# Moving six expert blocks of a mixture layer's first product from the dense stage into the stage before it

## The chip, the cores and the metric

One core of a Trainium2 chip runs the whole program. The metric is device time in microseconds (us) of one execution; the runs of a kernel are summed up by their median. The engines are named as the profile names them: PE (TensorE matmul) with PEld (its weight loads), DVE (VectorE), ACT (ScalarE), POOL (GpSimd) and SP (SyncE, which here only issues DMAs). Each engine takes its instructions in the order in which the program emits them.

## The reference

A bidirectional encoder block over 1024 tokens of width 1024: attention and a convolution side by side, then a retrieval layer with 16,384 experts, then a norm. Only the retrieval layer matters here. For each token, 8 heads pick 16 experts each, and the layer adds their outputs:

```
u = peer_u[e]
h = jax.nn.gelu(jnp.einsum('cd,chkd->chk', xc, u))
return jnp.einsum('chk,chkd->cd', g * h, peer_v[e])
```

`e` are the chosen experts of a token, found by two top-16 searches per head over 128 keys each and one over the candidate pairs; `g` is the softmax of the scores. All data are float32.

## The kernel before, in words

The 1024 tokens are 8 tiles of 128. Three tiles (`NG = 3`, 384 tokens) take the layer literally: for each of the 128 chosen experts of a token POOL issues an indirect DMA that fetches a row of `peer_u` or of `peer_v` per token (`rows` or `rx`, 128 rows of 4 KB), and DVE multiplies and adds it (L1195 for u, L1207 for v). That is 3 x 128 x 2 = 768 such gathers, each with one DVE instruction. Seven row buffers are in turn.

The other five tiles (640 tokens, `TD`) are computed densely. The experts are 128 blocks of 128. For a block i the first product is `gelu(peer_u[i] x HN)` (float32 split in a high and a low part, three products, so 48 matmuls of 320 columns; `HN` holds the 640 tokens), which is multiplied by a dense matrix of weights (`GD`, zero where a token has not chosen the expert) and multiplied with `peer_v[i]` (second product, 10 pieces of 128 tokens x 512 columns). Two stages concern us.

**The stage before the dense one** (the loop at L1410 on). Each turn of the loop does one group of the dense weights (`gpe`: eight matmuls `pg`, L1108, 160 groups in all; ACT evacuates them to `gblk`, and a DMA puts them into `GD` in DRAM after every eight groups) and one quarter of a first-product block (`ustep`: 12 matmuls, L1244). The finished block goes to DRAM (`HDm`). 31 blocks are made so (`KM = K0 - KT`, `K0 = 33`, `KT = 2`). With each turn `kadv` gives the top-16 searches and the gathers a credit of the turn's planned length, `max(dt + 1.4, 2.6)` with dt = 1.65 when a quarter was done and 0 otherwise; a gather costs 3.0 (`GCOST`), a step of the search what its generator yields. When the blocks are out the loop goes on with groups alone.

**The dense stage** starts with the two blocks left over (`KT`) and the loads for block 0. Then an iteration for each of blocks 0 to 126 does: loads for later blocks; `vsplit` of the next block's `peer_v` (ACT high part `vh`, POOL low part `vl`, L119); `uahead` (split of a `peer_uT` block for a first product to come, ACT and POOL, `uh` and `ul`, and the next load of one); and then three slots. A slot has a `rotate` (six matmuls into the one PSUM bank `prot`, which DVE then adds to X, L1569), `accum` (three matmuls in slots 1 and 2, six in slot 3, into four banks that stay), `ugroup` (12 matmuls, a quarter of a first product made here) and a few gathers. In the second slot `amake1` and `amake2` make the next block's left operand (DVE, `ho * gl`, L1487; ACT `ah`; DVE `al`). Of the 128 blocks 33 come back from `HDm` (`hload`); the other 95 are `ulist`, 380 quarters, one in each of 381 slots. SP issues all plain loads in the order of emission: `hload`, the `GD` slices `gl` (`gload`, every fourth block, both halves at once, three buffers), `vr` (`vload`), `ur` (`uload`).

Of the kernel before, what the change touches and what calls it, by code (L numbers as in the profile page):

```python
# [10 lines left out]
BF = mybir.dt.bfloat16  # L11
# [3 lines left out]
ALU = mybir.AluOpType  # L15
# [16 lines left out]
NK = 128  # L32
# [7 lines left out]
TB = 32  # L40
GCH = 4
NPERS = 4
K0 = 33
WIN = 2
NVI = 3
NO2 = 2
GPE = 1.4
GCOST = 3.0
KT = 2
GLAST = 1  # L50
FD = 2
# [20 lines left out]
def peer_block(tc, I, out):  # L72
    nc = tc.nc
    ctx = ExitStack()
    V, A, G, PE, SY = nc.vector, nc.scalar, nc.gpsimd, nc.tensor, nc.sync
# [1049 lines left out]
    class Gather:  # L1125
# [51 lines left out]
        def adv(self, n=1):  # L1177
            for _ in range(n):
                if not self.ready():
                    return  # L1180
                self.fill()
                ph, t, k = self.seq[self.nc]
                r = self.rows.pop(self.nc)
                self.nc += 1
                ps = self.ps
                if ph == 0:
                    h = self.h(t) if ps is None else ps
                    if k == 0:
                        self.hh[t] = gp.tile([P, P], F32, name=f"hh{t}")
                        if ps is not None:  # L1190
                            self.stage(t)
                            A.copy(ps, self.staged[t])
                            self.slots.append(self.staged.pop(t))
                    jk = QB[:, 2, :].bitcast(BF)
                    V.scalar_tensor_tensor(jk, r, 1.0, h, op0=ALU.mult, op1=ALU.mult,  # L1195
                                           accum_out=self.hh[t][:, k:k + 1])
                else:
                    if k == 0:
                        aa = gp.tile([P, P], F32, name=f"aa{t}")
                        A.activation(aa[:], self.hh[t][:], AF.Gelu_apprx_tanh)  # L1200
                        V.tensor_tensor(aa[:], aa[:], gg[t][:], op=ALU.mult)
                        self.aa[t] = aa
                    xt = X[:, t, :]
                    if k == 0 and ps is not None:
                        A.copy(ps, xt)
                    to = xt if ps is None else ps
                    V.scalar_tensor_tensor(to, r, self.aa[t][:, k:k + 1], to, op0=ALU.mult, op1=ALU.add)  # L1207
                    if k == P - 1 and ps is not None:
                        A.copy(xt, ps)
                self.slots.append(r)  # L1210
                if ph and k == P - 4 and t + 1 < NG and ps is not None:
                    self.stage(t + 1)
# [80 lines left out]
    def k_gat():  # L1293
        if not ks.get("gat") or not gat.ready():
            return None
        gat.adv(1)
        return GCOST

    def kstep():
        order = [("gen", k_gen), ("topk1", k_topk1), ("gat", k_gat)]  # L1300
# [49 lines left out]

    ust = dict(i=0, seg=0, hps=None, prev=None)

    def ustep():
        i = ust["i"]
        if i >= KM:
            return 0.0
        if i == 0 and ust["seg"] == 0:
            uload(US[0])
            uload(US[1])
            usplit(US[0])  # L1360
        sg = ust["seg"]
        if sg == 0:
            ust["hps"] = hbank([P, 2, 512], "hps")
        useg(US[i], ust["hps"], 2 * sg, 2 * sg + 2)
        if sg == 1 and ust["prev"] is not None:
            ho = gelu_(ust["prev"], up, 1)
            SY.dma_start(HDm[i - 1], ho[:])
        if sg == 1 and i < KM:
            usplit(US[i + 1])
            if i + 2 < K0:  # L1370
                uload(US[i + 2])
        ust["seg"] += 1
        if ust["seg"] == 4:
            ust["seg"] = 0
            ust["i"] += 1
            ust["prev"] = ust["hps"]
        return 1.65
# [34 lines left out]
    while True:  # L1412
# [4 lines left out]
            break  # L1417
        dt = max(dt + GPE * did, KB)
        kadv(dt, dt)
    ho = gelu_(ust["prev"], up, 1)  # L1420
    SY.dma_start(HDm[KM - 1], ho[:])
    while ks["n2"] < len(korder):
        clk["t"] += 2.0
        kstep()
# [2 lines left out]
    with ExitStack() as vs:  # L1427
# [27 lines left out]
        AL = {}  # L1455
        HO = {}

        def gload(i):
            for hf in range(2):
                gl[i, hf] = vp.tile([P, NB2, GCH, TB], F32, name="gl", tag="gl", bufs=3)  # L1460
                SY.dma_start(gl[i, hf][:], GD[hf * NB2:(hf + 1) * NB2, :, i:i + GCH, :].rearrange("b p i t -> p b i t"))

# [10 lines left out]
            CH[i] = (vh, vl)  # L1473

        hfree = [vp.tile([P, TD], F32, name=f"ho{j}")[:] for j in range(2)]
        hfree.append(QB[:, 0:2, :].rearrange("p a b -> p (a b)")[:, :TD])

        def hload(i):
            if i in UI and i not in HO and i < NK:
# [35 lines left out]

        def loads(i):
            if 0 <= i < NK:
                if i % GCH == 0:
                    gload(i)
                vload(i)  # L1520


        ulist = [i for i in range(NK) if i not in UI]
        ug = dict(g=0, split=0, load=0, ps=None)

        def uahead():
            m = ug["g"] // 4
            if ug["split"] < min(m + 2, len(ulist)):
                usplit(ulist[ug["split"]])
                ug["split"] += 1  # L1530
                if ug["load"] < len(ulist):
                    uload(ulist[ug["load"]])
                    ug["load"] += 1

        def ugroup():
            m, q = divmod(ug["g"], 4)
            if m >= len(ulist):
                return
            i, (hf, d) = ulist[m], divmod(q, 2)
            if ug["split"] <= m:  # L1540
                uahead()
            if d == 0:
                ug["ps"] = ubank()
            uhalf(i, hf, ug["ps"], d * DC // 2, (d + 1) * DC // 2)
            if d == 1:
                if hf == 0:
                    HO[i] = hfree.pop(0)
                ugelu(HO[i], hf, ug["ps"])
            ug["g"] += 1

        def uready(i):
            while i not in UI and ulist.index(i) >= ug["g"] // 4:
# [25 lines left out]
        ug["load"] = 2  # L1578
        hload(0)
        loads(0)  # L1580
        loads(1)
        for i in range(KM, K0):
            if i + 1 < K0:
                usplit(US[i + 1])
# [23 lines left out]
        for i in range(NK - 1):  # L1608
            nx = i + 1
            ng = gat0 + -(-(ngat - gat0) * min(nx, nb) // nb) - gat.nc  # L1610
            gs = [0] * 3
            for j in range(ng):
                gs[SPOTS[j % len(SPOTS)]] += 1
            hload(nx)
            if len(hfree) > 1:
                hload(i + 2)
            loads(i + 2)
            vsplit(nx)
            uahead()
            rs_ = [w for w in range(len(rot)) if i % WIN == w % WIN]  # L1620
            rotate(rs_[0], i, False)
            accum(i, (0,))
            ugroup()
            gat.adv(gs[0])
            rotate(rs_[1], i, False)
            accum(i, (1,))
            ugroup()
            uready(nx)
            amake1(nx)
            gat.adv(gs[1])  # L1630
            amake2(nx)
            rotate(rs_[2], i, False)
            accum(i, (2, 3))
            ugroup()
            gat.adv(gs[2])
            CH.pop(i - WIN, None)
        accum(NK - 1, range(len(pers)))
# [71 lines left out]
```

## Time and profile before

| | |
|---|---|
| runs, us | 2976.93 median of 3 (2971.88 to 2979.38) |
| profiled execution, us | 2979.52, its span 2977.7 |
| PE busy, share of the span | 94% |
| DVE busy | 81% |
| POOL busy | 64% |
| ACT busy | 39% |

A busy share is an average over stages; what a change in one of them is worth is read from that stage. Matmuls are pipelined, so that the durations of neighbouring ones overlap, and their spacing is less than their duration.

### The profile page before, as it was taken

The page shows a single profiled execution, that of the slowest core. Times are in us where ns is not written, and L with a number is a line of the kernel's source. Part 1 is how long each engine was busy: PE and PEld are TensorE (multiplying, and loading weights), DVE is VectorE, ACT ScalarE, POOL GpSimd, SP SyncE. Part 2 cuts the span into 40 slices and gives each one's busy share as a digit, 9 for nine tenths or more (in the row PEclk, how much of TensorE's full clock was granted, in tenths as well). Part 3 has the DMA queues.
Part 4 walks back from the last instruction along what each step waited for, and adds up shares of the span by engine and source line. Part 5 has one row for each costly group of instructions (what it writes and reads, how often), then busy time and mean ns, then how long its engine had stood idle before and what let it go on. Part 6 is the DMA issues. An engine that isn't in the chain of part 4 may idle for free.

```text
span 2977.7 us, 44502 instructions
## 1 busy us (share of the span) xinstructions
PE 2799.5 (94%) x16042; PEld 2477.2 (83%) x16048; DVE 2424.8 (81%) x4465; ACT 1166.3 (39%) x2408; POOL 1916.8 (64%) x1526
## 2 busy tenths in 40 slices
PE   7988899999999899978999999999999999999997
PEld 6867787798988788857888888888888888888886
DVE  4889877458666977766899988999889989898998
ACT  3237666243577577672222222222222222222222
POOL 2667741104446666765777777878777878787775
PEclk9999999899999999999999999999999999999999
DMA  3121000154345667668989898999989998999896
GB/s 124 53 76 36 1 15 1 53 161 122 96 149 181 224 219 251 235 238 299 342 331 350 328 348 331 345 342 352 337 319 337 344 343 336 347 336 339 332 342 227
DMA packets 296719, 710.33 MB, mean 239 GB/s; under 512 B 25264, under 2 KB 135216, under 8 KB 296368
## 3 DMA queue, kind: packets, MB, share of 16 engines
q0 software_dynamic: 110592, 402.70, 35.3%
q1 hardware_dynamic: 156800, 252.85, 25.2%
q10 hardware_dynamic: 29104, 51.91, 4.7%
q8 instruction: 126, 2.06, 0.3%
q14 instruction: 97, 0.79, 0.1%
HBM read 640.46 MB, written 66.91 MB: 238 GB/s over the span
## 4 chain that ended last, share of the span: by engine, by line
PE 53%; DVE 20%; DMA 11%; issue 7%; ACT 4%; POOL 4%; ACTq 1%; SPq 0%; POOLq 0%; DVEq 0%
PE hps L1504 13%; PE hps L1244 5%; PE prot L122 4%; PE prot L123 4%; PE prot L124 4%; DMA rows<-peer_u,ei 4%; PE pg L1108 3%; DMA rows<-peer_v,ei 2%; PE acc L124 2%; PE acc L122 2%; PE acc L123 2%; DMA vr<-peer_v 2%; DVE ga L1207 2%; DVE ho L1487 2%; DMA GD<-gblk 2%
## 5 line engine op out<-in xcount | busy, mean ns | idle before, releaser
L1504 PE MATMUL hps<-HN,uh 128*128 128x320 f32 x3072 | 682.8, 309 | 9.3 <-ACT ho L1251 5.3
L1504 PEld LDWEIGHTS hps<-HN,uh 128*128 128x128 f32 x3072 | 530.3, 188 | 42.7 <-issue 5.5
L1504 PE MATMUL hps<-HN,ul 128*128 128x320 f32 x1536 | 475.4, 309 | 0.6 <-POOL ul L119 0.6
L1207 DVE SCALAR_TENSOR_TENSOR ga<-rows,aa,ga 128x1024 f32<-128x1024 f32 x330 | 423.8, 1284 | 30.1 <-DMA rows<-peer_v,ei 23.6
L1162 POOL DMA_INDIRECT rows<-peer_u,ei x339 | 362.4, 1069 | 108.0 <-issue 56.3
L119 POOL TENSOR_TENSOR vl<-vr,vh 128x1024 fp32r<-128x1024 f32 x128 | 308.9, 2413 | 153.3 <-ACT vh L116 110.7
L1162 POOL DMA_INDIRECT rows<-peer_v,ei x330 | 325.2, 985 | 112.9 <-issue 64.5
L1195 DVE SCALAR_TENSOR_TENSOR QB<-rows,ga 128x1024 bf16<-128x1024 f32 x271 | 329.4, 1216 | 29.8 <-DMA rows<-peer_u,ei 25.5
L122 PE MATMUL prot<-vh,ah 128*128 128x512 f32 x762 | 308.8, 405 | 30.4 <-DVE X L1569 27.9
L119 POOL TENSOR_TENSOR ul<-ur,uh 128x1024 fp32r<-128x1024 f32 x127 | 323.0, 2543 | 2.6
L1569 DVE TENSOR_TENSOR X<-X,prot 128x512 f32<-128x512 f32 x384 | 261.9, 682 | 68.6 <-PE prot L124 66.4
L123 PE MATMUL prot<-vl,ah 128*128 128x512 f32 x762 | 301.0, 395 | 0.4 <-POOL vl L119 0.4
L124 PE MATMUL prot<-vh,al 128*128 128x512 f32 x762 | 297.4, 390 | 0.0
L1504 PEld LDWEIGHTS hps<-HN,ul 128*128 128x128 f32 x1536 | 289.1, 188 | 0.9 <-POOL ul L119 0.9
L1514 ACT ACTIVATE ho<-hps 128x320 f32<-128x320 f32 x128 | 55.9, 437 | 487.2 <-PE hps L1504 487.2
L1118 ACT COPY gblk<-pg 128x128 f32<-128x128 f32 x640 | 176.0, 441 | 100.6 <-PE pg L1108 71.4
L116 ACT CAST vh<-vr 128x1024 fp32r<-128x1024 f32 x128 | 133.7, 1045 | 201.7 <-DMA vr<-peer_v 201.7
L1244 PE MATMUL hps<-HN,uh 128*128 128x320 f32 x992 | 210.8, 335 | 0.0
L124 PE MATMUL acc<-vh,al 128*128 128x512 f32 x512 | 199.8, 390 | 0.0
L122 PE MATMUL acc<-vh,ah 128*128 128x512 f32 x512 | 199.8, 390 | 0.0
L123 PE MATMUL acc<-vl,ah 128*128 128x512 f32 x512 | 199.7, 390 | 0.0
L122 PEld LDWEIGHTS prot<-vh,ah 128*128 128x128 f32 x762 | 143.0, 188 | 67.9 <-DVE X L1569 47.6
(276 smaller groups left out, 6502.9 us busy)
## 6 DMA issues: line engine op xcount, KB each, us to landing
ur<-peer_uT SPq DMA_DIRECT2D x128, 512.0 KB, 4.4
vr<-peer_v SPq DMA_DIRECT2D x128, 512.0 KB, 7.8
GD<-gblk ACTq DMA_DIRECT2D x80, 512.0 KB, 5.1
gl<-GD SPq DMA_DIRECT2D x64, 640.0 KB, 7.7
wqr<-peer_wq SPq DMA_DIRECT2D x32, 512.0 KB, 3.9
HDm<-ho SPq DMA_DIRECT2D x31, 320.0 KB, 2.9
s<-SD SPq DMA_DIRECT2D x64, 128.0 KB, 3.0
ho<-HDm SPq DMA_DIRECT2D x22, 320.0 KB, 5.0
```

The lines of the kernel that those rows point to most:

```text
L116: A.copy(hi, src)
L119: lo_eng.tensor_tensor(lo, src, f(hi), op=ALU.subtract)
L122: PE.matmul(ps, ah, bh, start=start, stop=False)
L123: PE.matmul(ps, ah, bl, start=False, stop=False)
L124: PE.matmul(ps, al, bh, start=False, stop=stop)
L1118: A.copy(gblk[b][k][:, :, q * 4:q * 4 + 4].rearrange("p i t -> p t i"), pg[:, :, k * w:k * w + w])
L1162: G.indirect_dma_start(out=r, out_offset=None, in_=I["peer_v" if ph else "peer_u"], in_offset=bass.IndirectOffsetOnAxis(ap=ge[t][:, k:k + ...
L1195: V.scalar_tensor_tensor(jk, r, 1.0, h, op0=ALU.mult, op1=ALU.mult, accum_out=self.hh[t][:, k:k + 1])
L1207: V.scalar_tensor_tensor(to, r, self.aa[t][:, k:k + 1], to, op0=ALU.mult, op1=ALU.add)
L1244: PE.matmul(hps[:, j, :b - a], (uh, uh, ul)[st3][:, dc, :], HN[(0, 1, 0)[st3]][:, dc, a:b], start=dc == 0 and st3 == 0, stop=dc == DC - 1 ...
L1504: PE.matmul(ps[:, :b - a], (uh, uh, ul)[st3][:, dc, :], HN[(0, 1, 0)[st3]][:, dc, a:b], start=dc == 0 and st3 == 0, stop=dc == DC - 1 and ...
L1569: V.tensor_tensor(X[:, NG + t, n:n + 512], X[:, NG + t, n:n + 512], pr, op=ALU.add)
```

## The change

`K0` becomes 39, so 37 blocks are made in the loop of the stage before and 89 in the dense stage. A gather that is emitted after the last top-16 search costs 2.0 of credit instead of 3.0 (`GCOST2`). The product that L1195 writes beside its sum goes over the row itself instead of into a part of `QB`; with the space that this frees there are four buffers for finished blocks (`hfree`) instead of three. The last gelu of the loop is emitted in it (`ulast`). In the dense stage `gload` no longer stands ahead of `vload`: each half is loaded by itself, behind the `amake1` that reads the old one for the last time; `uload` stands behind `vload`; `uahead` splits behind the first quarter of a block; and the 356 quarters are spread over the 381 slots (`uslot`).

```
-K0 = 33
+K0 = 39
+GCOST2 = 2.0
...
-                    jk = QB[:, 2, :].bitcast(BF)
-                    V.scalar_tensor_tensor(jk, r, 1.0, h, op0=ALU.mult, op1=ALU.mult,
+                    V.scalar_tensor_tensor(r, r, 1.0, h, op0=ALU.mult, op1=ALU.mult,
                                            accum_out=self.hh[t][:, k:k + 1])
...
-        return GCOST
+        return GCOST if ks["n2"] < len(korder) else GCOST2
...
+    def ulast():
+        if ust["prev"] is not None:
+            ho = gelu_(ust["prev"], up, 1)
+            SY.dma_start(HDm[KM - 1], ho[:])
+            ust["prev"] = None
+
     def ustep():
         i = ust["i"]
         if i >= KM:
+            ulast()
             return 0.0
...
-        def gload(i):
-            for hf in range(2):
+        def gload(i, hf):
+            if i < NK:
...
-        hfree.append(QB[:, 0:2, :].rearrange("p a b -> p (a b)")[:, :TD])
+        hfree += [QB[:].rearrange("p a b -> p (a b)")[:, j * TD:(j + 1) * TD] for j in range(2)]
...
         def loads(i):
             if 0 <= i < NK:
-                if i % GCH == 0:
-                    gload(i)
                 vload(i)
...
         def uahead():
             m = ug["g"] // 4
             if ug["split"] < min(m + 2, len(ulist)):
                 usplit(ulist[ug["split"]])
                 ug["split"] += 1
-                if ug["load"] < len(ulist):
-                    uload(ulist[ug["load"]])
-                    ug["load"] += 1
+
+        def uloads():
+            if ug["load"] < min(ug["split"] + 2, len(ulist)):
+                uload(ulist[ug["load"]])
+                ug["load"] += 1
...
             ug["g"] += 1
+            if q == 0:
+                uahead()
+
+        def uslot():
+            ug["slot"] += 1
+            if ug["g"] < -(-4 * len(ulist) * ug["slot"] // (3 * (NK - 1))) and (ug["g"] % 4 != 1 or len(hfree) > 1):
+                ugroup()
...
         loads(0)
+        gload(0, 0)
+        gload(0, 1)
         loads(1)
+        gload(GCH, 0)
...
             hload(nx)
+            loads(i + 2)
             if len(hfree) > 1:
                 hload(i + 2)
-            loads(i + 2)
+            uloads()
             vsplit(nx)
-            uahead()
...
             amake1(nx)
+            if nx % GCH == GCH - 1:
+                gload(nx + 1, 1)
+                gload(nx + 1 + GCH, 0)
...
-            ugroup()
+            uslot()
```

(The last pair stands in each of the three slots.)

## Rows read from the trace of the kernel before

**Rows 1.** Stages: length, busy time of each engine (instructions), clock, DMA share, GB/s.

```profile
839.00:1277.60 438.60, 418.27 (x2843) 376.96 (x2843) 334.66 (x1199) 310.92 (x869) 284.24 (x230) 0.99 0.60 211
...
1277.60:1338.90 61.30, 44.25 (x260) 31.60 (x258) 38.61 (x50) 44.90 (x140) 33.99 (x22) 0.92 0.70 251
1338.90:1361.50 22.60, 16.10 (x96) 15.88 (x97) 3.04 (x4) 9.12 (x16) 1.56 (x1) 0.85 0.77 265
1361.50:2947.00 1585.50, 1559.79 (x8352) 1379.55 (x8353) 1427.54 (x1775) 387.98 (x547) 1232.71 (x918) 1.00 0.91 337
1900.00:2100.00 200.00, 199.95 (x1079) 177.78 (x1078) 181.98 (x270) 49.50 (x71) 159.25 (x120) 1.00 0.92 344
```

**Rows 2.** One quarter of a first product in the chain that ended last (start, us).

```profile
895.30 1.75 PE hps L1244 x12
```

**Rows 3.** Matmuls of the dense weights from 1140, and those from 1277.6 on.

```profile
L1108 PE MATMUL pg<-o,o x317: 270/275/275, 1139.8 to 1275.2; 128*128 128x128 f32 x159
...
L1108 PE MATMUL pg<-o,o x192: 270/275/582, 1277.7 to 1338.4; 128*128 128x128 f32 x192
```

**Rows 4.** A wait from 1277.6 to 1338.9: total us, times, longest.

```profile
PE pg L1108 <- ACT gblk L1118: 9.1, 2, 7.3
```

**Rows 5.** Gathers on DVE from 1277 to 1345 (ns min/median/max, first and last start).

```profile
L1195 DVE SCALAR_TENSOR_TENSOR QB<-rows,QB x17: 1214/1224/1226, 1277.1 to 1318.2; 128x1024 bf16<-128x1024 f32 x17
```

**Rows 6.** Dense stage by line: busy us, mean ns, idle before.

```profile
L1207 DVE SCALAR_TENSOR_TENSOR ga<-rows,aa,ga 128x1024 f32<-128x1024 f32 x327 | 419.9, 1284 | 30.1 <-DMA rows<-peer_v,ei 23.6 <-ACT ga L1205 1.5
...
L1569 DVE TENSOR_TENSOR X<-X,prot 128x512 f32<-128x512 f32 x380 | 259.1, 682 | 68.6 <-PE prot L124 66.4
...
L1487 DVE TENSOR_TENSOR ho<-ho,gl 128x320 f32<-128x320 f32 x169 | 172.3, 1058 | 3.0 <-DMA ho<-HDm 3.0
```

**Rows 7.** Waits of the dense stage: total us, times, longest.

```profile
ACT vh L116 <- DMA vr<-peer_v: 201.7, 32, 7.9
...
POOL vl L119 <- ACT vh L116: 110.7, 55, 4.8
...
DVE X L1569 <- PE prot L124: 62.9, 99, 2.0
...
DVE QB L1195 <- DMA rows<-peer_u,ei: 25.5, 28, 2.3
...
PE prot L122 <- DVE X L1569: 19.6, 44, 1.9
```

**Rows 8.** Waits of SP's queue in the dense stage.

```profile
SPq L1461 <- DVE ho L1487: 462.7, 21, 25.5
```

**Rows 9.** SP's queue in order of time, around 1675.

```profile
1674.79 21.83 SPq L1461 DMA_DIRECT2D gl<-GD  x2
1696.72 0.56 SPq L1465 DMA_DIRECT2D vr<-peer_v  x1
```

**Rows 10.** PE around the first and the last X addition of the 380.

```profile
1362.69 0.39 PE L124 MATMUL prot<-vh,al 128*128 128x512 f32 x1
...
2943.78 0.39 PE L124 MATMUL prot<-vh,al 128*128 128x512 f32 x1
2946.44 0.39 PE L122 MATMUL prot<-vh,ah 128*128 128x512 f32 x1
```

**Rows 11.** DVE: these two X additions.

```profile
1363.12 0.69 DVE L1569 TENSOR_TENSOR X<-X,prot 128x512 f32<-128x512 f32 x1 [3.55 <-PE prot L124]
...
2944.21 0.69 DVE L1569 TENSOR_TENSOR X<-X,prot 128x512 f32<-128x512 f32 x1 [0.61 <-PE prot L124]
```

**Rows 12.** DVE: two pairs of the multiplication by the dense weights.

```profile
1656.87 4.44 DVE L1487 TENSOR_TENSOR ho<-ho,gl 128x320 f32<-128x320 f32 x2
...
1683.24 0.89 DVE L1487 TENSOR_TENSOR QB<-QB,gl 128x320 f32<-128x320 f32 x2
```

**Rows 13.** POOL beside the first of these pairs.

```profile
1655.96 2.39 POOL L119 TENSOR_TENSOR vl<-vr,vh 128x1024 fp32r<-128x1024 f32 x1 [4.19 <-ACT vh L116]
1658.32 2.65 POOL L119 TENSOR_TENSOR ul<-ur,uh 128x1024 fp32r<-128x1024 f32 x1
```

More of the change, by code (lines that the diff above doesn't have):

```diff
@@ L1419, in peer_block @@
         kadv(dt, dt)
-    ho = gelu_(ust["prev"], up, 1)
-    SY.dma_start(HDm[KM - 1], ho[:])
+    ulast()
     while ks["n2"] < len(korder):
@@ L1517, in loads @@
             if 0 <= i < NK:
-                if i % GCH == 0:
-                    gload(i)
                 vload(i)
         ulist = [i for i in range(NK) if i not in UI]
-        ug = dict(g=0, split=0, load=0, ps=None)
+        ug = dict(g=0, split=0, load=0, ps=None, slot=1)
         def uahead():
@@ L1539, in ugroup @@
             i, (hf, d) = ulist[m], divmod(q, 2)
-            if ug["split"] <= m:
-                uahead()
             if d == 0:
@@ L1614, in peer_block @@
             hload(nx)
+            loads(i + 2)
             if len(hfree) > 1:
                 hload(i + 2)
-            loads(i + 2)
+            uloads()
             vsplit(nx)
-            uahead()
             rs_ = [w for w in range(len(rot)) if i % WIN == w % WIN]
@@ L1626, in peer_block @@
             accum(i, (1,))
-            ugroup()
+            uslot()
             uready(nx)
             amake1(nx)
+            if nx % GCH == GCH - 1:
+                gload(nx + 1, 1)
+                gload(nx + 1 + GCH, 0)
             gat.adv(gs[1])
@@ L1633, in peer_block @@
             accum(i, (2, 3))
-            ugroup()
+            uslot()
             gat.adv(gs[2])
```

## The prediction

> **What bounds the kernel now.** I read the stages first [rows 1]. In the dense stage (1361.5 to 2947.0, 1585.5 us of a span of 2977.7) PE is busy 1559.8 us: it sets the pace and stands still for 25.7 us only. DVE follows closely with 1427.5 us, DMA with a share of 0.91. In the last stretch before it (1277.6 to 1338.9) PE has no first product left, is busy 44.3 of 61.3 us, and DVE only 38.6. Taking work out of the dense stage and putting it into this stretch is the core of the change. The waits come next [rows 4, 7, 8]: what still holds PE in the dense stage is almost only DVE's addition that frees `prot` (19.6 us in 44 waits), and DVE in turn waits 62.9 us for PE. The two run nearly in step, one `prot` bank apart. Last, single slots in order of time [rows 9 to 13].
>
> **Part 1, six blocks out of the dense stage.** A quarter of a block is 12 matmuls in 1.75 us [rows 2], a block 7.0 us, six blocks 42 us of PE time. With all stalls unchanged the dense stage is 42 us shorter.
>
> **Part 2, six blocks into the loop before.** Behind the last quarter 192 matmuls of the dense weights are left [rows 3], at 8 a turn 24 turns. Six blocks are 24 quarters: they go just into turns that exist, and no turn is added. What such a turn costs with a quarter in it is seen just before: 317 matmuls from 1139.8 to 1275.2 are 39.6 turns in 136.3 us, 3.44 us each. 24 x 3.44 = 82.6 us against the 61.3 us that these turns take now [rows 1]: **+21.3 us**. So half of the 42 us is paid back here; the gain is only the 17 us in which PE stands still and what the matmuls lose at the lower clock of 0.92. Below: from 839 on PE is busy 418.3 of 438.6 us [rows 1]; a turn with none of that idle time is 3.28 us, which gives +17.5. The wait of 7.3 us for the evacuation of the dense weights [rows 4] is inside the 61.3 and goes with the longer turn. Above: the bytes. In the 24 turns there will be 12 stores of `GD` at 0.52 MB, 6 blocks of `peer_uT` at 0.52, 6 results at 0.33 and 27 gathers at 0.52 (next part): 25.6 MB in 82.6 us, 310 GB/s, more than the 251 of now [rows 1] but less than the 344 seen later. In the second half, with the gathers at their densest, I count about 370; the excess over 344 in 45 us is 3.5 us, so +26.
>
> **Part 3, cheaper gathers.** A turn earns 2.6 of credit now, and 3.05 with a quarter in it. The 24 turns earn 62.4 now, of which 17 gathers [rows 5] take 51 and the rest of the last search 11.4: six steps of 1.8 and a little, and since a gather stands between two steps, seven of the 17 are spent beside the search. After: 73.2; 11.4 for the search and 21 for those seven leave 40.8, at 2.0 each 20 gathers, so 27 instead of 17. Ten fewer are left to the dense stage. DVE does one in 1.28 us [rows 6], so 13 us leave DVE's 1427.5. PE does not get shorter by it; the hiding place in the loop is DVE's idle time there [rows 1].
>
> **Part 4, the stretch between.** From the last matmul of the dense weights to the first `rotate` it is 22.6 us [rows 1], PE busy 16.1 with the two left-over blocks. After, the chain is the same: gelu, last evacuation, split of the last block, `gl` and `vr`, the left operand. One gelu comes earlier by the new place of `ulast`; `gl` is issued one load later. I take 0, bounds -4 and +5 (a late tail of gathers in front of DVE's split).
>
> **Part 5, empty slots.** 356 quarters in 381 slots leave 25 slots without one; following the counters, 23 stand inside the stage, 16 in slots 1 and 2 and seven in slot 3. There the cover for the X addition is gone. From the end of one `rotate` to the next 2.27 us pass (2943.78 + 0.39 to 2946.44 [rows 10]), of which the quarter is 1.76; without it 0.51 us are left (1.2 in slot 3, which has three accumulating matmuls more). The addition ends 0.73 us after the end of its `rotate` when DVE is free, at the first and at the last one [rows 10, 11]. Over all 380, from 1363.12 to 2944.21, I took the same difference: median 1.16 us, a quarter of them over 2.33. Setting each against the shorter cover gives a mean stall of 0.73 to 0.83 us by slot, say 0.8: 23 x 0.8 = **+18 us**. Bounds: 16 x 0.22 = 4 (DVE always free) and 23 x 1.75 = 40 (nothing of a quarter is kept).
>
> **Part 6, the order of the loads.** Now SP stands in front of a `gl` for 21.8 us, and `vr` behind it goes out at 1696.72 [rows 9]; over the stage 463 us in 21 waits [rows 8], and a third less often behind the `QB` buffer. What is late next: ACT waits 201.7 us for `vr`, POOL 110.7 us for `vh`, and behind `vl` in POOL's queue stand the gathers, so that DVE waits some 50 us for rows [rows 6, 7]; then the X addition is late and PE waits. After, `vr` goes out before the halves of `gl`, and `uload` waits for a split of an earlier iteration. It can take back at most the 25.7 us that PE stands still; nothing at least. Most of these stalls sit in short waits spread over all iterations, not only in each fourth, so I take a third: **-9 us**.
>
> **Part 7, costs nothing.** L1195 writing over its row: DVE's instruction remains of 1024 elements; the row buffer was held until its end anyway. HDm: six stores and six loads more (0.33 MB each), six `ur` less (0.52): 1 MB less on the queues of the dense stage. The fourth buffer only removes waits. The longer PE queue of the loop is POOL's too (cast and subtraction of six blocks more), hidden in its 27 us of idle time there [rows 1]; uncovered, it would be six times 3.5 us, 21 us.
>
> **The sum.** 2979.5 (the profiled execution) - 42 + 21 + 0 + 18 - 9 = 2967.5, that is -12. The median of the runs shown is 2.6 us below that execution; 2976.9 - 12 = **2965**.
>
> **Rivals.** *Loads free the stage.* If the late `vr` is behind nearly all stalls, and DVE with ten gathers less is free in time, the dense stage falls by 50: PE at 1518 plus 17. For: DVE's 62.9 us of waiting for PE is slack. Against: 337 GB/s x 1585.5 us are 534 MB, some 528 after; at 344 GB/s, which is what the stage moved in its best 200 us with PE busy 199.95 [rows 1], that takes 1535, so no more than 50 fits there. Time: 2977 - 50 + 21 = 2948.
>
> *DVE inherits the pace.* The stalls stay as they are and an empty slot gives back 0.8 to 1.1 us: dense stage -17 to -24. Time: 2977 - 21 + 21 = 2977, no change. For: the two engines are in step now. Against: of DVE's 158 us of idle time 95 are not for PE; with its 1415 us of work that makes 11.9 us for each of 127 iterations, just under PE's 1518/127 = 11.95.
>
> *Slower: POOL stands in DVE's way.* A pair of L1487 takes 0.89 us when POOL computes nothing, 4.44 when it falls together with `vl` and `ul` [rows 12, 13]; the mean of one is 1.06 us [rows 6], twice the free 0.45. The change moves `ul` from right behind `vl` to behind a first quarter, nearer to `amake1`. If that makes pairs collide more often, DVE's 11.9 us an iteration rises by two times the rise of the mean; from 12.31 (the old 1585.5/127 = 12.48 less the loop's 21 us over 127) the kernel is slower, that is from a mean of 1.27 on. At 1.35 the iteration is 12.48, the dense stage is as long as now and the kernel takes 2977 + 21 = 2998. Against: two separate subtractions block for 2.4 us at most each, where the pair of them blocks for 5, and six `ul` less are run. The Trainium skill (SBUF — State Buffer, "Who interferes with whom") states it as a rule: a VectorE instruction with two SBUF inputs and a GpSimd instruction that reads SBUF exclude each other for a whole instruction. The trace agrees, with 4.44 us beside 0.89; by that rule alone the sign of the move is open, since which of them starts first decides.
>
> **How the numbers follow.** Chances: the forecast (net -5 to -19) 0.47, loads free the stage (-20 to -33) 0.16, no change 0.25, slower 0.12. A measurement of this kernel can tell about 0.3% (9 us). Some 0.34 of the forecast's chance lie beyond it, the rest within: faster 0.34 + 0.16 = 0.50, same 0.13 + 0.25 = 0.38, slower 0.12. The range: down to 2944 (the freed stage with a loop of +18), up to 2986 (no change, with the loop at +26 and the stretch between at +5): it leaves out most of the slower case. The forecast alone would be 2958 to 2972.
>
> **What would show it.** Right: the loop's 24 turns last 80 to 86 us with no gap of PE; ten gathers more before the dense stage; a dense stage of 1545 to 1560 us; PE's waits for DVE's X addition up from 20 to 30 to 40 us, in slots without a quarter; SP's waits in front of `gl` no longer ahead of a `vr`, and ACT's wait for `vr` far under 200. Wrong: PE's idle time in the dense stage under 18 us (empty slots cost nothing), or a mean of L1487 over 1.27 us with DVE over 93% busy (POOL), or turns longer than 3.7 us (bytes).

## The result, and the profile after

The changed kernel takes **2949.5 us** (median of 6 runs, 2947.15 to 2952.67), the one before 2972.06 us beside it (6 runs). The ratio is 0.9918, 95% interval 0.9900 to 0.9937: faster, by 22.6 us (0.8%) at the medians. Forecast were 2965 us and a gain of 12; the range of 2944 to 2986 holds the time, but the forecast gain is only about half of the measured one. Of the 15.5 us between forecast and time, 4.9 are the start: the forecast started from a median of 2976.9 for the kernel before.

The stages of the kernel after, to be set against [rows 1]; columns as there (length, busy time of each engine with instructions, clock, DMA share, GB/s). They are the loop from its first first-product matmul to its last matmul, its last 24 turns, the stretch between, and the dense stage:

```profile
838.30:1362.80 524.50, 498.53 (x3389) 449.68 (x3387) 395.24 (x1264) 362.79 (x1013) 357.04 (x272) 0.99 0.64 224
1276.50:1362.80 86.30, 80.70 (x546) 72.56 (x544) 60.09 (x68) 51.99 (x145) 69.50 (x43) 0.98 0.82 292
1362.80:1387.30 24.50, 14.58 (x97) 14.09 (x97) 3.03 (x4) 7.71 (x15) 1.58 (x1) 0.94 0.87 291
1387.30:2914.60 1527.30, 1508.66 (x8062) 1338.00 (x8063) 1346.71 (x1757) 375.42 (x529) 1207.52 (x903) 1.00 0.95 345
```

The loop takes 524.5 us for 499.4 before (from its first first-product matmul at 839.3 on), the stretch between 24.5 for 22.8, the dense stage 1527.3 for 1585.5: +25.1, +1.7, -58.2. The sum, -31.4, is more than the -22.6 of the medians, because a profile is one execution: the one of the kernel before, 2979.5 us, is 7.5 above its median, the one after, 2947.15, is 2.4 below. In which stages these 10 us lie can't be seen, so a difference to the stages of the kernel before can be wrong by some us. The stages ahead of the loop, which nobody touched, ended anywhere from 830.6 to 840.0 in the kernels below. So stages are compared with stages here, and totals only by medians and ratios.

The dense stage by line, answering to [rows 6] (lines have moved: L1569 is L1580 now, L1487 is L1493, L1495 is L1501, L122 to L124 are L123 to L125, L1504 is L1510):

```profile
L1207 DVE SCALAR_TENSOR_TENSOR ga<-rows,aa,ga 128x1024 f32<-128x1024 f32 x326 | 418.9, 1285 | 8.4 <-DMA rows<-peer_v,ei 1.9 <-DVE aa L1201 0.6 <-ACT ga L1205 0.6
...
L1580 DVE TENSOR_TENSOR X<-X,prot 128x512 f32<-128x512 f32 x380 | 260.0, 684 | 125.4 <-PE prot L125 104.3 <-issue 20.5
...
L1493 DVE TENSOR_TENSOR QB<-QB,gl 128x320 f32<-128x320 f32 x126 | 84.5, 711 | 0.0
L1493 DVE TENSOR_TENSOR ho<-ho,gl 128x320 f32<-128x320 f32 x127 | 76.6, 643 | 0.1
```

The multiplication by the dense weights fell from a mean of 1.06 us to 0.64 and 0.71, and DVE no longer waits for rows (1.9 us for 23.6). Its work in the stage fell by 81 us (1427.5 to 1346.7), of which the nine u gathers that went into the loop are 11. The waits, answering to [rows 7]:

```profile
DVE X L1580 <- PE prot L125: 104.3, 149, 3.8
...
PEld prot L123 <- DVE X L1580: 29.0, 33, 3.5
POOL vl L120 <- ACT vh L117: 28.4, 24, 2.3
...
ACT vh L117 <- DMA vr<-peer_v: 25.2, 15, 4.7
...
PE prot L123 <- DVE X L1580: 16.7, 16, 3.1
```

ACT's wait for `vr` fell from 201.7 us to 25.2, POOL's for `vh` from 110.7 to 28.4. The two engines have changed sides: DVE waits for PE 104.3 us, 3.8 of them ahead of the first addition, instead of 62.9 without that first wait. SP's queue in order of time, at the place of [rows 9]:

```profile
1703.51 0.33 SPq L1226 DMA_DIRECT2D ur<-peer_uT  x1
1711.46 1.85 SPq L1467 DMA_DIRECT2D gl<-GD  x2
1713.40 4.56 SPq L1471 DMA_DIRECT2D vr<-peer_v  x1
```

`gl` is issued 1.85 us after SP comes to it here, no longer 21.83. Over the whole stage SP still stands in front of `gl` for 328 us in 31 waits, for 670 in 31 before, but what stands behind it now is not urgent: ACT waits 25.2 us for `vr`.

### The profile page after: what moved, and what is told of

Read it like the earlier page. It is cut to its first block, busy times and chain, and to the rows that moved or that the text cites. A ratio compares the mean times of both kernels' runs of the same rounds, so it can differ in the third digit from the quotient of the medians.

```text
span 2945.4 us, 44232 instructions
## 1 busy us (share of the span) xinstructions
PE 2783.8 (95%) x16048; PEld 2474.3 (84%) x16048; DVE 2367.2 (80%) x4465; ACT 1159.5 (39%) x2396; POOL 1930.6 (66%) x1532
## 3 DMA queue, kind: packets, MB, share of 16 engines
q1 hardware_dynamic: 158528, 256.79, 25.7%
## 4 chain that ended last, share of the span: by engine, by line
PE 69%; DVE 16%; issue 5%; ACT 4%; DMA 3%; POOL 2%; ACTq 1%; SPq 0%; POOLq 0%; DVEq 0%
PE hps L1510 19%; PE hps L1244 6%; PE prot L123 6%; PE prot L124 5%; PE prot L125 5%; PE acc L123 3%; PE acc L124 3%; PE acc L125 3%; PE pg L1109 3%; DVE y L152 2%; DVE ac L152 1%; DVE PT L120 1%; DVE mx L712 1%; DVE ga L1207 1%; PE pqT L123 1%
## 5 line engine op out<-in xcount | busy, mean ns | idle before, releaser
L1510 PE MATMUL hps<-HN,uh 128*128 128x320 f32 x2880 | 638.0, 308 | 3.2 <-ACT gblk L1119 1.8
L1510 PEld LDWEIGHTS hps<-HN,uh 128*128 128x128 f32 x2880 | 496.8, 188 | 32.0 <-issue 2.0
L1510 PE MATMUL hps<-HN,ul 128*128 128x320 f32 x1440 | 445.1, 309 | 0.0
L1580 DVE TENSOR_TENSOR X<-X,prot 128x512 f32<-128x512 f32 x384 | 262.7, 684 | 125.4 <-PE prot L125 104.3
L120 POOL TENSOR_TENSOR vl<-vr,vh 128x1024 fp32r<-128x1024 f32 x128 | 309.5, 2418 | 57.5 <-ACT vh L117 28.4
L123 PE MATMUL prot<-vh,ah 128*128 128x512 f32 x762 | 306.2, 402 | 33.1 <-DVE X L1580 24.5
L1195 DVE SCALAR_TENSOR_TENSOR rows<-rows,ga 128x1024 f32<-128x1024 f32 x264 | 313.2, 1214 | 6.7 <-ACT ga L1193 4.6
L124 PE MATMUL prot<-vl,ah 128*128 128x512 f32 x762 | 302.5, 397 | 0.0
L125 PE MATMUL prot<-vh,al 128*128 128x512 f32 x762 | 298.1, 391 | 0.0
L1510 PEld LDWEIGHTS hps<-HN,ul 128*128 128x128 f32 x1440 | 270.4, 188 | 0.0
L1520 ACT ACTIVATE QB<-hps 128x320 f32<-128x320 f32 x88 | 38.5, 438 | 467.4 <-PE hps L1510 373.4
L1520 ACT ACTIVATE ho<-hps 128x320 f32<-128x320 f32 x90 | 39.4, 438 | 457.0 <-PE hps L1510 342.5
L1244 PEld LDWEIGHTS hps<-HN,uh 128*128 128x128 f32 x1184 | 195.3, 191 | 21.7 <-issue 0.8
L123 PE MATMUL acc<-vh,ah 128*128 128x512 f32 x512 | 199.9, 390 | 0.0
L124 PE MATMUL acc<-vl,ah 128*128 128x512 f32 x512 | 199.7, 390 | 0.0
L125 PE MATMUL acc<-vh,al 128*128 128x512 f32 x512 | 199.6, 390 | 0.0
```

The costliest lines, as they stand in the source:

```text
L120: lo_eng.tensor_tensor(lo, src, f(hi), op=ALU.subtract)
L123: PE.matmul(ps, ah, bh, start=start, stop=False)
L124: PE.matmul(ps, ah, bl, start=False, stop=False)
L125: PE.matmul(ps, al, bh, start=False, stop=stop)
L1195: V.scalar_tensor_tensor(r, r, 1.0, h, op0=ALU.mult, op1=ALU.mult, accum_out=self.hh[t][:, k:k + 1])
L1244: PE.matmul(hps[:, j, :b - a], (uh, uh, ul)[st3][:, dc, :], HN[(0, 1, 0)[st3]][:, dc, a:b], start=dc == 0 and st3 == 0, stop=dc == DC - 1 ...
```

## The experiments

Twelve kernels, each in a batch with its own runs of the kernel before; ratios are to those. The first question was whether the order of the loads carries the gain, and some other part gives time back, or the six blocks with the cheaper gathers carry it; the later ones settle what gives time back. Each expectation names its own theories.

**Without the six blocks** (`K0 = 39` back to `33`, all else as changed).

> The changed kernel with K0 = 33 again: the six blocks go back into the dense stage (95 of its own, 380 quarters in 381 slots), everything else stays as changed. Theory A (the new order of loads and splits keeps DVE early, whatever the number of blocks): the loop before the dense stage gets its 21 to 25 us back, the dense stage is 42 us longer than after the change less the 7 us that empty slots cost there, PE's idle time in it stays under 15 us and DVE waits under 10 us for rows; total about 2949.5 - 24 + 35 = 2961, ratio to before 0.996. Theory B (the gain is that of the six blocks, the order brings nothing): PE's 25 us of idle time return as well, total 2972 to 2976, ratio 1.00.

2943.5 us, ratio 0.9911 (0.9891 to 0.9932): as fast as the whole change, and below the 2961 us of A. The dense stage is 1548.6, the loop 505.1. So in this kernel the six blocks bring nothing: 21 us out of the dense stage, 19 into the loop.

**`gl` first again**, all else as changed:

```diff
         def loads(i):
             if 0 <= i < NK:
+                if i % GCH == 0:
+                    gload(i, 0); gload(i, 1)
                 vload(i)
...
-            if nx % GCH == GCH - 1:
-                gload(nx + 1, 1)
-                gload(nx + 1 + GCH, 0)
```

> The changed kernel with both halves of gl loaded ahead of vr again, every fourth iteration. Theory A (vr behind a waiting gl made the gathers and then the X addition late): ACT's wait for vr goes from 25 us back towards 200, DVE's wait for rows from 4 us back towards 50, PE's idle time in the dense stage from 18 us to 35 or more; total 2962 to 2972, ratio 0.997 to 1.0. Theory B (the order of the plain loads does not matter, since DVE has slack; the place of the POOL split does it): vr is late again, but the total stays at 2949 to 2954, ratio 0.992 to 0.994.

3020.6 us, ratio 1.0155 (1.013 to 1.018), **slower than before** and beyond both theories. ACT waits 201.2 us for `vr` again, as in [rows 7], and the dense stage is 1607.6.

**The split where it was**, behind `vsplit`:

```diff
         def ugroup():
+            if ug["split"] <= m:
+                uahead()
...
-            if q == 0:
-                uahead()
...
             vsplit(nx)
+            uahead()
```

> The changed kernel with the split of a peer_uT block back behind vsplit at the start of an iteration, so that POOL computes vl and ul one right after the other. Theory A (load order alone): total stays at 2949 to 2954; the mean of L1493 may rise from 0.68 us to 1.0 us without effect, as PE sets the pace. Theory B (two subtractions one after the other block DVE's pairs): the mean of L1493 goes from 0.68 back to about 1.05 us, DVE's busy time in the dense stage from 1347 us to some 1425, empty slots cost 0.5 us and more instead of 0.1 to 0.4, total 2958 to 2968, ratio 0.995 to 0.999.

2934.1 us, ratio 0.9881 (0.9856 to 0.9905); dense stage 1515.9. Neither theory had it faster than the change: the split's new place seems to cost time.

**The gathers' old price in the loop** (`GCOST2 = 3.0`, all else as changed).

> The changed kernel with a cost of 3.0 for every gather (as before). Theory A (PE sets the pace in the loop and in the dense stage, so the gathers' place costs nothing): about six gathers return to the dense stage, DVE does 8 us more there out of its 104 us of waiting for PE; total within 3 us of 2949.5, ratio 0.991 to 0.993. Theory B (bytes: the loop's last 24 turns move 292 GB/s and the dense stage 345, so gathers matter): the loop is 2 to 4 us shorter and the dense stage 6 to 10 us longer, total 2952 to 2957.

2930.5 us, ratio 0.9856 (0.983 to 0.9882), faster than either theory gave. The loop is 3.8 us shorter, as expected from one of them, but the dense stage, which has to do the six gathers more (71 are done in the loop, 77 in the changed kernel), is 9 us shorter too and not longer.

**The changed kernel again**, as a control in the second batch.

> The changed kernel once more, as it is, beside the other kernels of this batch, so that they can be compared on one chip: 2946 to 2953, ratio 0.990 to 0.994, unless the stages before 830 to 840 us, which the change does not touch and which differ by up to 9 us between executions, move it.

2948.4 us, ratio 0.9911 (0.9897 to 0.9925). Loop 524.9, between 24.2, dense 1531.2: two executions of one kernel differ by about 4 us in the dense stage, and by little elsewhere behind 838.

**Both** (the split of `e3_split_old` and `GCOST2 = 3.0`).

> The changed kernel with the split back behind vsplit and with a cost of 3.0 for every gather. Theory A (each of the two took its own time: the split made al collide with POOL, the ten gathers lengthened the loop and shifted the gathers in the dense stage): the gains of e3 (11 us in the dense stage) and e4 (9 in the dense stage, 4 in the loop) add up in part; loop 521, dense stage 1508 to 1514, total 2920 to 2928, ratio 0.982 to 0.985. Theory B (both moved the same thing, DVE's position when a gather changes from u to v): no more than one of them, dense stage 1515 to 1519, total 2928 to 2935.

2922.9 us, ratio **0.9830** (0.9817 to 0.9843), as A had it: the two costs add up. It is the fastest of all, and beats both kernels.

**The order of `gl` alone, in the kernel before**:

```diff
-        def gload(i):
-            for hf in range(2):
+        def gload(i, hf):
+            if i < NK:
...
-                if i % GCH == 0:
-                    gload(i)
...
         loads(0)
+        gload(0, 0)
+        gload(0, 1)
         loads(1)
+        gload(GCH, 0)
...
             amake1(nx)
+            if nx % GCH == GCH - 1:
+                gload(nx + 1, 1)
+                gload(nx + 1 + GCH, 0)
```

> The kernel before with one thing changed: the two halves of gl are loaded where the change loads them, behind the last use of the old ones, so that no vr stands behind a waiting gl. Six blocks, four buffers, empty slots, split and upload order stay as before. Theory A (this alone is the gain): ACT's wait for vr from 202 us to under 60, DVE's wait for rows from 50 to under 10, the dense stage from 1586 to 1545 to 1555, total 2935 to 2945, ratio 0.986 to 0.991. Theory B (uload, which waits 698 us for POOL on the same queue, holds vr just as well, and its move is needed): wait for vr stays over 100 us, dense stage over 1570, ratio 0.994 to 1.0.

2935.2 us, ratio 0.9879 (0.9863 to 0.9895): -37 us by twelve lines, **more than by the whole change** (0.9911 in the same batch; the intervals just don't touch). Nothing else differs from the kernel before, so its dense stage shows what a late `vr` did. The stage, then its groups, then its waits:

```profile
1356.00:2902.30 1546.30, 1540.95 (x8352) 1380.59 (x8353) 1330.80 (x1775) 386.66 (x547) 1235.05 (x918) 1.00 0.93 345
```

```profile
L1567 DVE TENSOR_TENSOR X<-X,prot 128x512 f32<-128x512 f32 x380 | 260.5, 686 | 135.2 <-PE prot L124 132.6
L1487 DVE TENSOR_TENSOR ho<-ho,gl 128x320 f32<-128x320 f32 x169 | 96.8, 611 | 3.9 <-DMA ho<-HDm 2.1 <-DMA gl<-GD 1.8
```

```profile
POOL vl L119 <- ACT vh L116: 41.1, 51, 3.4
...
ACT vh L116 <- DMA vr<-peer_v: 12.0, 12, 2.7
...
PEld prot L122 <- DVE X L1567: 8.0, 12, 1.8
...
PE prot L122 <- DVE X L1567: 4.9, 8, 1.5
```

To be seen is a chain. `vr` in time (12.0 us of waiting for 201.7) lets POOL do `vl` and `ul` earlier, and they collide less with `amake1`: the same 169 instructions of L1487 take 0.61 us each instead of 1.06. Of all 253 instructions of that line 118 overlap a subtraction of POOL in the kernel before, with a mean of 1.70 us (the others 0.48); here 70 do, with 0.99. With them DVE's work falls by 97 us at equal instructions, more than its waits for rows, which fall from 55 us to 30 and not under 10 as A had it. The X addition is in time, and PE waits for it 4.9 us instead of 19.6. The chain is argued from the trace; no run changes the collisions alone. The stage falls by 39.2 us, though PE stood still for 25.7 us only, and this was the surprise. PE's weight loads have the answer; the first row is of the kernel before, in its dense stage:

```profile
PEld prot L122 <- DVE X L1569: 38.9, 73, 2.1
PEld hps L1504 <- ACT ho L1514: 4.6, 6, 1.4
PEld hps L1504 <- ACT QB L1514: 3.6, 5, 1.3
```

A stall of PE begins at the weight load in front of the matmul, and all of them together were 50.4 us, which the new order takes down to 12.8. At the matmul a part of a stall shows as idle time (25.7 to 5.3 us), and the other part as "busy" time: the same 8352 matmuls are booked with 1559.8 us before and with 1541.0 here.

**No six blocks, old split** (`e3_split_old` with `K0 = 33`).

> The changed kernel with K0 = 33 and the split back behind vsplit: beside e3 it says what the six blocks bring when nothing collides with al. Theory A (the blocks are worth their 42 us in the dense stage when DVE keeps up): dense stage 1545 to 1550 (PE never waits, it cannot go lower), so that e3's 1516 is 30 us under it against 19 us that the loop costs: six blocks bring about 10 us; total 2940 to 2946. Theory B (the blocks bring nothing, whatever the split): total 2930 to 2936, as e3.

2940.3 us, ratio 0.9892 (0.9879 to 0.9906), dense stage 1542.9, loop 505.1: the total of A, at its lower end, with a dense stage 2 us under A's. Beside `e3_split_old` the six blocks bring 6 us at the medians, and the intervals overlap. With 33 blocks the split's place matters little (0.9911 in `e1_k33`), and the loop is 5.6 us longer than the 499.5 of `e6_before_gl`, with as many quarters in it, but with the cheaper gathers.

**Gathers dearer still** (`e5_both` with `GCOST2 = 6.0`).

> Kernel e5 (split back, gathers at 3.0) with a cost of 6.0 for a gather behind the last search: 40.8 of credit are about 7 gathers there instead of 13 (at 2.0 it is 20). Theory A (the gathers in the last 24 turns crowd the stores of GD, which the turns wait for, and the dense stage takes them for nothing): the loop goes from 519.9 to 515 to 518, the dense stage stays at 1509 to 1514, total 2917 to 2921. Theory B (what cheaper gathers lost was their own place in the dense stage, not the loop): the loop stays at 520, the dense stage is 3 to 6 us longer, total 2925 to 2930.

2931.6 us, ratio 0.9849 (0.983 to 0.9868), not told apart from `e5_both`. The loop gives back 1.2 us and the dense stage takes 5.7, nearer to B. So nothing speaks for a price above 3, though a difference of 5.7 in one profile is little more than two executions differ by.

**`gl` first in the best kernel** (`e5_both` with the edit of `e2_gl_first`).

> Kernel e5 with both halves of gl ahead of vr again, so all of the change but its order of gl, its split and its cheaper gathers. Theory A (the price of an empty slot hangs on DVE: with vr late it is the 0.8 us that was predicted from the old trace): loop 520, dense stage 1586 - 42 + 18 = 1562, within 1552 to 1572; mean of L1493 about 1.05 us; DVE waits 40 us and more for rows; total 2963 to 2983, no faster than the kernel before. Theory B (empty slots cost 0.3 us in any case): dense stage 1540 to 1550, total 2950 to 2960. Theory C (with gl first, the new place of uload makes vr later than it ever was before, as in e2): dense stage 1590 and more, total over 3000.

3003.5 us, ratio 1.0098 (1.0074 to 1.0122), dense stage 1588.5: more than A gave, and but for 1.5 us in the dense stage what C did. C's reason isn't borne out: ACT waits 194.6 us for `vr`, no more than the 201.7 of the kernel before. So the order is worth 77 us of the dense stage here, where it was worth 39 in the kernel before:

```profile
PE prot L123 <- DVE X L1583: 29.5, 35, 2.3
PE hps L1510 <- ACT QB L1520: 14.6, 4, 7.0
PE hps L1510 <- POOL ul L120: 10.3, 5, 3.4
PE hps L1510 <- ACT ho L1520: 5.1, 1, 5.1
```

The last three, 30 us, are waits of the first product itself, which were 4.6 us at the matmul in the kernel before: to judge by them, blocks made just in time suffer from a late load directly. Another part is TensorE's clock. In this dense stage the granted clock stands at its lower level, 0.5 of 2.4 GHz, for 42.3 us in nine stretches, the eight inside the stage each behind or within a pause of PE of 1.8 to 7.0 us; in `e5_both` it does for 5.8 us, at the start alone. At half the clock that is some 18 us of the 77, an estimate from these two lengths. In the kernel before and in `e6_before_gl` it stands there for 3.4 us each, so those 39 us have no such part.

```profile
1371.90:2960.40 1588.50, 1527.76 (x8062) 1348.55 (x8063) 1388.76 (x1769) 378.05 (x529) 1211.32 (x909) 0.99 0.91 334
```

**Quarters as early as they fit** (`e5_both` without the even spreading over the slots):

```diff
-            if ug["g"] < -(-4 * len(ulist) * ug["slot"] // (3 * (NK - 1))) and (ug["g"] % 4 != 1 or len(hfree) > 1):
+            if ug["g"] % 4 != 1 or len(hfree) > 1:
```

> Kernel e5 (changed kernel, split back, gathers at 3.0) without the even spreading: a quarter goes into every slot as long as a buffer for a finished block is free. By the counters 19 slots stay empty before the last two blocks, all of them slot 2, and six in these two. Theory A (with DVE early an empty slot costs 0.3 us, wherever it lies): dense stage 1508 to 1516, total 2918 to 2928, as e5. Theory B (spreading is needed, since what is empty in a row at the end leaves PE under DVE's pace, and the loads of ur come in bursts): dense stage 1520 and more, total over 2930.

2931.8 us, ratio 0.9867 (0.9841 to 0.9893); dense stage 1519.9: B's total, and all but B's dense stage. The spreading may be worth 9 us; the intervals just touch.

**`uload` where it was** (`e5_both` with the load right behind the split, in `uahead`).

> Kernel e5 with the load of a peer_uT block right behind a split again, as before the change (SP then waits there for the subtraction of that split: 698 us in 62 waits in the kernel before). Theory A (only gl ahead of vr hurt; a wait that ends with POOL's subtraction holds vr for less than it can bear, as in e6): dense stage 1509 to 1516, total 2919 to 2928. Theory B (uload's place is part of the gain): ACT waits over 80 us for vr, dense stage 1520 and more, total over 2930.

2971.3 us, ratio 0.9992 (0.9976 to 1.0008): all of the gain is gone, as B had it. SP's queue in the dense stage:

```profile
SPq L1226 <- POOL ul L120: 835.4, 81, 20.9
SPq L1471 <- POOL vl L120: 176.2, 29, 9.5
SPq L1467 <- DVE ho L1493: 120.9, 28, 11.5
```

`ur` needs the buffer that POOL's `ul` has just been given to read, so SP stands there for up to 20.9 us, with `vr` behind it: ACT waits 109.3 us for `vr`. In `e6_before_gl` the same place is harmless, though SP stands there for longer in total (929.6 us, 14.9 at most). There a quarter is in every slot; whether that is the reason wasn't tried.

## Why the prediction was right or wrong

The stages of the kernels with the most telling differences, from the profiled executions (us):

| kernel | loop | between | dense | ratio |
|---|---|---|---|---|
| before | 499.4 | 22.8 | 1585.5 | 1 |
| order of `gl` alone | 499.5 | 25.1 | 1546.3 | 0.9879 |
| and six blocks, buffers, `uload`, spreading (`e5_both`) | 519.9 | 23.5 | 1511.8 | 0.9830 |
| and `GCOST2` of 2.0 (`e3_split_old`) | 524.6 | 23.5 | 1515.9 | 0.9881 |
| or the split's new place (`e4_gcost3`) | 520.7 | 23.7 | 1518.4 | 0.9856 |
| and both (the change; control in brackets) | 524.5 (524.9) | 24.5 (24.2) | 1527.3 (1531.2) | 0.9918 (0.9911) |

**Part 6, the order of the loads (-9): this step failed most.** It measured -39 us by itself (-37 at the medians). The chain begins and ends as it was described, with `vr` and with the X addition that PE waits for. Its middle was another: of DVE it saw only the waits for rows, which fell by 24 us, and not the work, which fell by 97 with the collisions of L1487; those the forecast had left to a rival. And the bound was wrong. "At most the 25.7 us that PE stands still" took PE's idle time for its stalls, and the weight loads showed 50.4 us. And a third of the bound was taken because the stalls were spread over all iterations, not only each fourth. But they were not: an undisturbed slot takes 3.82 us from the start of one `rotate` to the next (4.50 as slot 3), and of the 47.6 us that the slots of the kernel before take above that, every fourth iteration (2, 6, 10, ...) holds 1.1 and the three behind it 46.5. In `e6_before_gl` 8.3 us are left in all, and the difference of 39.3 is the whole fall of the stage.

**Part 5, empty slots (+18): too large, in part for the same reason.** The stall was worked out from the additions of the kernel before, which ended 1.16 us (median) after their `rotate`, a quarter of them later than 2.33. Over the same 380 additions it is 0.73 and 1.22 in the changed kernel and 0.73 and 1.18 in `e5_both`: with DVE early the lag is the free one of 0.73 that [rows 10, 11] show. An empty slot in the changed kernel:

```profile
1694.06 0.39 PE L125 MATMUL prot<-vh,al 128*128 128x512 f32 x1
...
1694.74 0.39 PE L125 MATMUL acc<-vh,al 128*128 128x512 f32 x1
1695.23 0.50 PE L123 MATMUL prot<-vh,ah 128*128 128x512 f32 x1
```

```profile
1694.49 0.69 DVE L1580 TENSOR_TENSOR X<-X,prot 128x512 f32<-128x512 f32 x1
```

The `rotate` ahead of it ended at 1694.45 and the next starts 0.78 us later, where 0.51 would do: 0.27 us for an empty slot 1 or 2, close to the lower bound of 0.22. Of the 17 such slots in the trace 13 take 0.78. All 24 empty slots together, with the seven in slot 3, stand 10.7 us above their covers in the changed kernel, 5.2 in `e5_both` and 10.3 in `e9_both_gl_first`, where DVE is late: in none of them 18.

**Part 2 (+21.3) was right, part 1 (-42) too large.** Where only `K0` differs the loop grows by 19.5 us (`e7_k33_split_old` to `e3_split_old`) and 19.4 (`e1_k33` to the change), but the dense stage falls by 27.0 and 21.3. What failed is "with all stalls unchanged". What the slots with a quarter take above the undisturbed 3.82 and 4.50 us goes from 5.0 us to 13.4 in the first pair and from 10.6 to 21.4 in the second. 42 less this rise and less the empty slots (7.2 and 10.7) makes 26 and 21. So parts 1 and 5 together, -24, came out near the measured values by luck in part: half of the stalls lie in slots that kept their quarter, which neither part speaks of. At the medians the blocks bring 6 us in the first pair, where the intervals overlap, and nothing in the second. From the order alone to `e5_both` the dense stage falls by 34.5, the loop grows by 20.4 and the median falls by 12 (2935.2 to 2922.9); but there the buffers, `uload` and the spreading change as well.

**Part 3, cheaper gathers: the count was right, the price left out.** Nine more are done in the loop (77 for 68; ten were expected), six of them by the new price. No cost was set against it; the price costs the loop 4.7 us (`e5_both` to `e3_split_old`) and 3.8 (`e4_gcost3` to the change), and the whole kernel, by the ratios of the same pairs (the second to the control), 15 and 16 us of 2973; the intervals don't touch. The loop's +25 lies near the +26 that was the bound for too many bytes, with the last turns at 292 GB/s; whether it is the bytes wasn't tried. That the dense stage is not shorter by it (+4 and +9 to +13, the first no more than two executions differ by) has no shown cause.

**The rival "POOL stands in DVE's way": the mechanism was right, at another instruction.** The watch was on L1487, and its mean fell. What is hit is `al`, which follows it: with the split in its new place two groups of `al` take 1086 and 1021 ns (changed kernel), and with the old place 821 and 822 (`e5_both`). Of the 126 `al` 18 overlap a subtraction of POOL in the changed kernel, with a mean of 2.45 us, and the other 108 take 0.82; in `e5_both` none overlaps one.

```profile
L1501 DVE TENSOR_TENSOR al<-QB,ah 128x640 fp32r<-128x640 f32 x63 | 68.4, 1086 | 16.8 <-ACT ah L1495 9.3 <-issue 4.4 <-ACT ho L1520 2.8
L1501 DVE TENSOR_TENSOR al<-ho,ah 128x640 fp32r<-128x640 f32 x63 | 64.3, 1021 | 17.4 <-ACT ah L1495 11.2 <-issue 4.2 <-ACT ho L1520 0.8
```

```profile
L1501 DVE TENSOR_TENSOR al<-ho,ah 128x640 fp32r<-128x640 f32 x63 | 51.8, 822 | 13.9 <-ACT ah L1495 13.8
L1501 DVE TENSOR_TENSOR al<-QB,ah 128x640 fp32r<-128x640 f32 x63 | 51.7, 821 | 12.2 <-ACT ah L1495 12.2
```

One of these collisions in order of time, POOL, DVE and PE of the changed kernel:

```profile
2074.46 2.37 POOL L120 TENSOR_TENSOR ul<-ur,uh 128x1024 fp32r<-128x1024 f32 x1 [3.20 <-ACT uh L117]
```

```profile
2074.64 2.87 DVE L1501 TENSOR_TENSOR al<-QB,ah 128x640 fp32r<-128x640 f32 x1
2077.44 0.68 DVE L1580 TENSOR_TENSOR X<-X,prot 128x512 f32<-128x512 f32 x1
```

```profile
2078.16 0.50 PE L123 MATMUL prot<-vh,ah 128*128 128x512 f32 x1 [2.47 <-DVE X L1580]
```

`al` starts 0.18 us behind POOL's `ul` and ends 0.68 us behind it: 2.87 us for 0.82. The addition stands behind `al`, and PE loses 2.47 us in a slot with a quarter. By the ratios the new place costs 8 us without the cheap gathers (`e5_both` to `e4_gcost3`, whose intervals overlap) and 9 with them (`e3_split_old` to the control, where they just touch); the dense stage is 7 and 11 to 15 us longer. The Trainium skill (SBUF — State Buffer, "Who interferes with whom") has the rule by which a VectorE instruction with two SBUF inputs and a GpSimd instruction that reads SBUF shut each other out; these rows agree with it, 2.87 us beside 0.82.

**The rival "loads free the stage" (2948)** came nearest in time, for half of its reason: the late `vr` was behind 39 of the 47.6 us of stalls, and the dense stage fell by 58, not 50, even with 16 given back by the split's place and the gathers' price. Its ceiling of 344 GB/s was none: `e5_both` moves 351 over its whole dense stage:

```profile
1374.80:2886.60 1511.80, 1504.66 (x8062) 1337.27 (x8063) 1323.80 (x1770) 376.54 (x529) 1209.60 (x909) 1.00 0.95 351
```

**Part 4 and the 24 turns** came out near the forecast (+1.7 for 0, within -4 to +5; 86.3 us for 82.6, just over the 80 to 86, and PE is busy for 80.7 of them where no gap was foretold). **Part 7** holds for L1195 and the buffers; its sentence on what uncovered POOL work would cost didn't think of the split's place.

By the measured terms of the dense stage: -39 for the order, -35 for the blocks and what was changed with them, +16 for the split's place and the cheap gathers together, which makes -58; and +25 and +2 ahead of it. Forecast were -33 and +21. That the time lies in the range is luck in part: the order brought 30 us more than its term, and the two parts that were put at nothing took 16 of them back. Of the prediction's own signs, ACT's wait for `vr` and (but for one) the gathers came; the dense stage, 1527 for 1545 to 1560, and PE's waits for the X addition, 16.7 for 30 to 40, did not.

What stays open: why the single stalls behind a late `gl` are longer in the new schedule than in the old one, and why the cheap gathers lengthen the dense stage.

## What to carry to other kernels

A plain load that has to wait for its buffer holds back every load behind it in an in-order queue, so issue it behind the instruction that frees its buffer, and not ahead of a load that is needed sooner: here this was worth more than moving 42 us of PE's work to another stage. Read the stalls of TensorE at its weight loads and not from its idle time, and don't cost a new schedule with lags measured while another engine is late for a reason that the same change removes. Measure each edit of a bundle alone; two parts of this one, a moved split and a cheaper credit, cost 24 us of the 50 that were to be had (ratio 0.9911 for 0.9830).

## What the runs showed of the hardware

A stall can cost PE more than its length. In the changed kernel, around 1511 us (windows as above, first the stall, then the three us after it, then the next):

```profile
1507.60:1511.00 3.40, 0.44 (x2) 0.02 (x1) 2.78 (x5) 1.76 (x2) 1.02 (x1) 0.96 0.96 360
1511.10:1514.30 3.20, 3.20 (x8) 2.55 (x9) 3.13 (x3) 0.00 (x0) 1.56 (x3) 0.52 0.65 195
1514.30:1518.00 3.70, 3.70 (x22) 3.35 (x21) 3.66 (x4) 0.44 (x1) 3.52 (x3) 1.00 0.80 256
```

Behind 3.05 us without a matmul the granted clock is 0.52, about the lower of its two levels (1.2 GHz), for 3.2 us, and eight matmuls are done in them, most at a distance of 0.43 us for the 0.23 of full clock. That is some 1.3 us more (3.12 us for eight times 0.23), booked as busy time. The stage's mean clock is still 1.00 to two digits: only a short window shows it. Not every pause is followed by one: behind the 2.47 us at 2078 the matmuls stand 0.23 us apart again from the second one on.
